# One 512-column matmul for both parts of an activation, in a hybrid RWKV-7, latent attention and ConvFFN layer

## The chip, the core and the metric

The kernel runs on one core of a Trainium2 chip. Its engines work side by side, each with an instruction queue of its own: TensorE (PE, with its weight loads PEld), VectorE (DVE), ScalarE (ACT), GpSimd (POOL) and SyncE (SP), which issues most DMAs. The metric is the device time of one execution in microseconds; lower is better. TensorE's granted clock is 2.4 GHz or 1.2 GHz; the profile shows it as 1.00 or 0.50.

## What is computed

One layer on 256 latent tokens and 256 context tokens of 2048 features. Cut to what matters here:

```python
def token_mixer(h, s0, ang, kv_prefix, P, emit):
    p = h @ P['w_in']
    p_rwkv, p_mla, p_gate = jnp.split(p, [RWKV_IN, RWKV_IN + MLA_IN], axis=-1)
    y_rwkv, s_fin = rwkv_branch(p_rwkv, s0, P, emit)
    k, v = mla_kv(p_mla, P, ang)
    ...
    o = blocked_attention(q, k_all, v_all).reshape(B, T, MLA_HEADS * V_HEAD)
    g_rwkv, g_mla = jnp.split(jax.nn.sigmoid(p_gate + P['gate_b']), N_BRANCH, axis=-1)
    merged = g_rwkv * (y_rwkv @ P['w_rwkv_proj']) + g_mla * (o @ P['w_mla_proj'])
    return merged @ P['w_out'], s_fin, (k, v)

def conv_ffn(h, P):
    u = depthwise_conv(h @ P['ffn_w_gate'], P['ffn_conv_w'], P['ffn_conv_b'])
    return (jax.nn.gelu(u, approximate=True) * (h @ P['ffn_w_val'])) @ P['ffn_w_down']

# the layer
x = x + g1 * rms_norm(out_lat, norm_mix_post)
h = modulate(rms_norm(x, norm_ffn_pre), sh2, sc2)
x = x + g2 * rms_norm(conv_ffn(h, P), norm_ffn_post)
```

## The kernel before

Features lie on partitions, tokens along the free axis: a product is 128 output features by 256 tokens in one PSUM bank, summed over K tiles of 128 input features. To keep float32 accuracy with the fast float32r matmuls, each operand is cut into two float32r parts, hi + lo. `weights` (line 151) loads up to 1024 weight columns (8 K tiles) by a DMA on SP and cuts each 512 of them, hi by a cast on ACT (line 186), lo by a subtraction on DVE (line 187), into a ring of five pairs of tiles `whi` and `wlo`. `gemm` (line 165) then issues three matmuls for a K tile: hi by hi (line 176), hi by the activation's lo (179), lo by hi (180). All products of the program go through `gemm`, but for the values of the attention (`values`, lines 902 to 904) and the heads' outputs (999 to 1001), which issue the same three by hand. The activations' parts are two separate tiles: `hc` and `hl` (normed context and latents), `ckv`, `cq`, `o`, `yg`, `mg`, `z`, `f`.

The stages, in order of time: `start` (modulation, first norm, the first seven units of 128 columns of `w_in`), then keys and values of the context, then `branches` (line 755): the other columns of `w_in`, the attention and its projection (`pm`) run in the foreground, and between their K tiles `pump` steps background generators, the RWKV pairs' three stages and, behind each pair, `finish` (line 714: group norm, which sends sums through DRAM and back). Then `merge` (`pr`, which reads the finished pairs back from DRAM as `yg`), the output projection (`project`, tile `o_ps`), `second_norm`, `ffn` (tile `pf`: 44 pairs of units, gate and value) and the down projection (`project` again). The order of each queue is made by a scheduler that simulates the program: an instruction's place follows from the order of the code and from when its operands are there in that simulation.

`second_norm` (line 1093) does not wait for the norm's 1/rms R: z is the residual stream x1 times the gains, without R, in two parts, with the modulation's shift as two more columns (so a matmul has 258). The six products of the first three pairs (`first`) start on it in quarters of K, while the sum of squares is made; `rst_pr` holds R on all partitions after two small matmuls, and ACT copies it to `R_o`. `ffn` multiplies each unit's columns by R (line 1157 or 1166) and adds the shift's column `col`:

```python
            pu, col = unit("w_fg", i)
            ...
            nc.vector.tensor_tensor(c, pu, R, ALU.mult)
            nc.scalar.activation(up[:, 1:257], c, AF.Identity, bias=col)
```

## Time and profile before

| | us |
|---|---|
| median of three runs | 2328.25 |
| lowest, highest | 2321.64, 2334.10 |
| span of the profiled execution (from its first to its last instruction) | 2325.7 |

The profile is of one execution. Its time is given as the span; what a run's time has beside the span is not in the profile. A group's "idle before" is the engine's idle time just ahead of its instructions, with the engine or DMA that ended it. Ends of matmuls are modelled and overlap the next one's start, so steps are taken from start to start; a stretch counts every instruction that lies in it in part.

### The profile page before, as it was taken

The page shows a single profiled execution, that of the slowest core. Times are in us where ns is not written, and L with a number is a line of the kernel's source. Part 1 is how long each engine was busy: PE and PEld are TensorE (multiplying, and loading weights), DVE is VectorE, ACT ScalarE, POOL GpSimd, SP SyncE. Part 2 cuts the span into 40 slices and gives each one's busy share as a digit, 9 for nine tenths or more (in the row PEclk, how much of TensorE's full clock was granted, in tenths as well). Part 3 has the DMA queues.
Part 4 walks back from the last instruction along what each step waited for, and adds up shares of the span by engine and source line. Part 5 has one row for each costly group of instructions (what it writes and reads, how often), then busy time and mean ns, then how long its engine had stood idle before and what let it go on. Part 6 is the DMA issues. An engine that isn't in the chain of part 4 may idle for free.

```text
span 2325.7 us, 50524 instructions
## 1 busy us (share of the span) xinstructions
PE 2225.3 (96%) x18728; PEld 2079.7 (89%) x18728; DVE 1542.7 (66%) x2970; ACT 1204.0 (52%) x2536; POOL 616.6 (27%) x1555
## 2 busy tenths in 40 slices
PE   5999989899999999999999999979999999999996
PEld 2788989898999998888877999979999999999996
DVE  5258677766756767777767457579686868655554
ACT  3244455555555556656655335546555555554442
POOL 0100016655655655465545000011010100000000
PEclk9999999999999999999999999989999999999998
DMA  9979787767767659778566578538575757556663
GB/s 349 317 232 304 234 280 229 226 190 215 231 192 220 212 163 305 247 245 266 174 195 178 172 234 294 176 112 281 182 254 182 254 175 246 181 178 184 188 185 111
DMA packets 250454, 511.39 MB, mean 220 GB/s; under 512 B 44800, under 2 KB 104208, under 8 KB 249568
## 3 DMA queue, kind: packets, MB, share of 16 engines
q1 hardware_dynamic: 246368, 501.88, 67.7%
q0 software_dynamic: 3840, 6.30, 1.1%
q8 instruction: 147, 2.41, 0.4%
q14 instruction: 99, 0.81, 0.1%
HBM read 455.54 MB, written 52.53 MB: 218 GB/s over the span
## 4 chain that ended last, share of the span: by engine, by line
PE 64%; DMA 5%; POOL 5%; DVE 3%; issue 2%; ACT 1%; SPq 0%; DVEq 0%; POOLq 0%; ACTq 0%
PE pf L176 7%; PE pf L179 7%; PE pf L180 7%; PE o_ps L179 5%; PE o_ps L176 5%; PE o_ps L180 5%; POOL Z L637 2%; POOL Zt L635 2%; PE g L180 2%; PE g L176 2%; PE g L179 2%; PE y_ps L708 1%; PE u_ps L691 1%; DMA lanes<-ti_d 1%; PE x_ps L685 1%
## 5 line engine op out<-in xcount | busy, mean ns | idle before, releaser
L187 DVE TENSOR_TENSOR wlo<-raw,whi 128x512 fp32r<-128x512 f32 x1072 | 740.1, 697 | 368.8 <-ACT whi L186 343.3
L186 ACT CAST whi<-raw 128x512 fp32r<-128x512 f32 x1072 | 654.2, 619 | 449.0 <-PE o_ps L179 135.5
L176 PE MATMUL pf<-z,whi 128*128 128x258 f32 x1408 | 401.8, 286 | 4.6 <-ACT z L1111 4.6
L180 PE MATMUL pf<-z,wlo 128*128 128x258 f32 x1408 | 399.5, 285 | 3.2 <-DVE wlo L187 3.2
L179 PE MATMUL pf<-z,whi 128*128 128x258 f32 x1408 | 400.9, 285 | 1.2 <-DVE z L1112 1.2
L176 PE MATMUL g<-hl,whi 128*128 128x256 f32 x1120 | 330.5, 295 | 1.1 <-ACT whi L186 0.6
L180 PE MATMUL g<-hl,wlo 128*128 128x256 f32 x1120 | 326.8, 293 | 1.6 <-DVE wlo L187 1.5
L179 PE MATMUL g<-hl,whi 128*128 128x256 f32 x1120 | 323.9, 289 | 0.0
L176 PEld LDWEIGHTS pf<-z,whi 128*128 128x128 f32 x1408 | 269.0, 191 | 4.9 <-ACT z L1111 4.9
L180 PEld LDWEIGHTS pf<-z,wlo 128*128 128x128 f32 x1408 | 267.9, 191 | 3.7 <-DVE wlo L187 3.7
L179 PEld LDWEIGHTS pf<-z,whi 128*128 128x128 f32 x1408 | 269.7, 192 | 1.5 <-DVE z L1112 1.5
L635 POOL TENSOR_TENSOR Zt<-Z,lanes 128x60 f32<-128x60 f32 (+24 forms) x496 | 194.2, 392 | 131.2 <-DMA lanes<-ti_d 71.5
L180 PEld LDWEIGHTS g<-hl,wlo 128*128 128x128 f32 x1120 | 218.5, 196 | 7.4 <-DVE wlo L187 2.6
L176 PEld LDWEIGHTS g<-hl,whi 128*128 128x128 f32 x1120 | 218.9, 195 | 6.3 <-issue 2.5
L179 PEld LDWEIGHTS g<-hl,whi 128*128 128x128 f32 x1120 | 219.0, 196 | 3.1 <-issue 1.2
L338 DVE SCALAR_TENSOR_TENSOR adacc<-araw,c,adacc 128x512 f32<-128x512 f32 x240 | 181.2, 755 | 53.5 <-DMA araw<-w_ada 51.7
L637 POOL TENSOR_TENSOR Z<-Z,Zt 128x60 f32<-128x60 f32 (+24 forms) x496 | 204.3, 412 | 36.0
L179 PE MATMUL o_ps<-f,whi 128*128 128x256 f32 x704 | 198.1, 281 | 0.0
L176 PE MATMUL o_ps<-f,whi 128*128 128x256 f32 x704 | 198.1, 281 | 0.0
L180 PE MATMUL o_ps<-f,wlo 128*128 128x256 f32 x704 | 198.1, 281 | 0.0
L1090 POOL TENSOR_TENSOR raw_o<-raw_o,R_o 128x1024 f32<-128x1024 f32 x2 | 4.7, 2347 | 489.6 <-ACT R_o L1083 489.6
L179 PEld LDWEIGHTS o_ps<-f,whi 128*128 128x128 f32 x704 | 132.5, 188 | 0.0
(327 smaller groups left out, 4826.7 us busy)
## 6 DMA issues: line engine op xcount, KB each, us to landing
raw<-w_in SPq DMA_DIRECT2D x150, 512.0 KB, 5.2
araw<-w_ada SPq DMA_DIRECT2D x256, 256.0 KB, 4.7
raw<-w_fg SPq DMA_DIRECT2D x82, 512.0 KB, 3.9
raw<-w_fv SPq DMA_DIRECT2D x82, 512.0 KB, 4.2
raw<-w_down SPq DMA_DIRECT2D x80, 512.0 KB, 3.7
araw<-w_ada SPq DMA_DIRECT2D x64, 512.0 KB, 6.0
raw<-w_mla SPq DMA_DIRECT2D x32, 512.0 KB, 4.7
raw<-w_out SPq DMA_DIRECT2D x32, 512.0 KB, 4.6
```

What stands on the lines that cost most here:

```text
L176: mm = nc.tensor.matmul(ps, wh, ahi[:, k], start=k == 0 and not shared, stop=False)
L179: nc.tensor.matmul(ps, wh, alo[:, k], start=False, stop=False)
L180: nc.tensor.matmul(ps, wl, ahi[:, k], start=False, stop=k == kt - 1 and (not shared or ps is segs[-1][0]))
L186: cut = self.nc.scalar.copy(hi, src)
L187: self.nc.vector.tensor_tensor(lo, src, hi.bitcast(F32), ALU.subtract)
L338: nc.vector.scalar_tensor_tensor(acc, raw, self.c1[:, k:k + 1], acc, ALU.mult, ALU.add)
L635: nc.gpsimd.tensor_tensor(tm[:, :m, j + 1:], Z[:, :m, j:j + 1].broadcast_to([128, m, t]), N[:, j:j + 1, j + 1:].broadcast_to([128, m, t]), ...
L637: nc.gpsimd.tensor_tensor(Z[:, :m, j + 1:], Z[:, :m, j + 1:], tm[:, :m, j + 1:], ALU.subtract)
L685: nc.tensor.matmul(px[64:128, u], XS[u // 2][:, c, u % 2], st[:, u], start=True, stop=True)
L691: nc.tensor.matmul(pu[64:128, u], vu[64:128, u], xv[64:128, u], start=True, stop=True)
L708: nc.tensor.matmul(o, st[64:128, u], rt[:, d, e, c], start=False, stop=True)
L1090: mul = eng.tensor_tensor(raw[:, c], raw[:, c], R.rearrange("p (o t) -> p o t", o=1).broadcast_to([128, 4, 256]), ALU.mult)
```

## The change

`hi` and `lo` of a weight become one tile `wc` of [128, 2, 512]. The two parts of an activation become one tile with, for each K tile, hi and lo side by side: [128, k, 2, 256]. A product's PSUM tile becomes 512 columns wide (it had half of a bank, now it has all). `product`, which `gemm`, `values` and `head` now call, looks at the widths: where PSUM is twice the activation it issues one matmul of 512 columns, weight hi by both parts, and one of 256, weight lo by the activation's hi, into the first half; otherwise the three matmuls of before. The latter holds for `start`'s units, for the three first pairs of up projections and for the keys `kn_ps`, whose activation has 512 tokens. `take` adds the two halves of a PSUM tile: a copy on ACT and an addition on DVE; every reader of a product now goes through it. `second_norm` still makes z, now in the end of the tile `f`, for the first three pairs, and then makes `h`, the normed and modulated input itself, in two parts: x1 times R (two quarters on DVE, two on POOL, into `raw`), times the gains plus the shift on DVE, and the split. The pairs from the fourth on read `h`, and need neither R nor the shift's column. The comments are taken out, so lines have other numbers. The core of the diff:

```diff
             pool, bufs = next(self.cuts)
-            hi = pool.tile([128, 512], F32R, tag="whi", name="whi", bufs=bufs)
-            lo = pool.tile([128, 512], F32R, tag="wlo", name="wlo", bufs=bufs)
-            cut = self.split(hi, lo, raw[:, o:o + 512])
+            w = pool.tile([128, 2, 512], F32R, tag="wc", name="wc", bufs=bufs)
+            cut = self.split(w[:, 0], w[:, 1], raw[:, o:o + 512])
             if HOLD and len(self.heads) >= HOLD:
                 self.behind(cut, self.heads[-HOLD])
-            yield hi, lo
+            yield w
...
-            for i, (hi, lo) in enumerate(self.weights(src[:, k0 * 128:(k0 + kn) * 128], kn * 128)):
-                for ps, ahi, alo in segs:
+            for i, w in enumerate(self.weights(src[:, k0 * 128:(k0 + kn) * 128], kn * 128)):
+                for ps, act in segs:
                     for j in range(4):
                         k = k0 + 4 * i + j
-                        wh, wl = hi[:, j * 128:j * 128 + 128], lo[:, j * 128:j * 128 + 128]
-                        mm = nc.tensor.matmul(ps, wh, ahi[:, k], start=k == 0 and not shared, stop=False)
+                        wh, wl = w[:, 0, j * 128:j * 128 + 128], w[:, 1, j * 128:j * 128 + 128]
+                        mm = self.product(ps, wh, wl, act[:, k], k == 0 and not shared, k == kt - 1 and (not shared or ps is segs[-1][0]))
                         if j == 0:
                             head = mm
-                        nc.tensor.matmul(ps, wh, alo[:, k], start=False, stop=False)
-                        nc.tensor.matmul(ps, wl, ahi[:, k], start=False, stop=k == kt - 1 and (not shared or ps is segs[-1][0]))
...
+    def product(self, ps, sh, sl, act, start, stop):
+
...
+        mm = self.nc.tensor.matmul
+        n = act.shape[2]
+        if ps.shape[1] == 2 * n:
+            m = mm(ps.rearrange("p (i n) -> p i n", i=2), sh, act, start=start, stop=False)
+            mm(ps[:, 0:n], sl, act[:, 0], start=False, stop=stop)
+            return m
+        m = mm(ps, sh, act[:, 0], start=start, stop=False)
+        mm(ps, sh, act[:, 1], start=False, stop=False)
+        mm(ps, sl, act[:, 0], start=False, stop=stop)
+        return m
+
+    def take(self, out, ps, rows=slice(0, 128)):
...
+        self.nc.scalar.copy(out, ps[rows, 0:256])
+        if ps.shape[1] == 512:
+            self.nc.vector.tensor_tensor(out, ps[rows, 256:512], out, ALU.add)
+
...
-        segs = [(self.psg.tile([128, 256], F32, tag="g", name="g"), *(self.hc if s == "c" else self.hl)) for s in seqs]
+        segs = [(self.psg.tile([128, 512], F32, tag="g", name="g"), self.hc if s == "c" else self.hl) for s in seqs]
         self.gemm(self.a["w_in"][t], KT, segs, pump=pump)
         return [s[0] for s in segs]
...
-        nc.scalar.activation(g, ps, AF.Tanh, bias=self.gbh[:, i:i + 1], scale=0.5)
+        self.take(g, ps)
+        nc.scalar.activation(g, g, AF.Tanh, bias=self.gbh[:, i:i + 1], scale=0.5)
         nc.sync.dma_start(self.gsc[i], g)
...
-            pr = self.psg.tile([128, 256], F32, tag="g", name="pr")
-            self.gemm(self.a["w_rwkv"][i], 8, [(pr, *yg)])
+            pr = self.psg.tile([128, 512], F32, tag="g", name="pr")
+            self.gemm(self.a["w_rwkv"][i], 8, [(pr, yg)])
             m = ep.tile([128, 256], F32, tag="mm", name="mm", bufs=2)
-            nc.vector.scalar_tensor_tensor(m, gt[:, 0], 1.0, pr, ALU.add, ALU.mult)
+            self.take(m, pr)
+            nc.vector.scalar_tensor_tensor(m, gt[:, 0], 1.0, m, ALU.add, ALU.mult)
             nc.vector.tensor_tensor(m, m, gt[:, 1], ALU.add)
-            nc.scalar.mul(self.mg[0][:, i], m, 0.5)
-            nc.vector.scalar_tensor_tensor(self.mg[1][:, i], m, 0.5, self.mg[0][:, i].bitcast(F32), ALU.mult, ALU.subtract)
+            nc.scalar.mul(self.mg[:, i, 0], m, 0.5)
+            nc.vector.scalar_tensor_tensor(self.mg[:, i, 1], m, 0.5, self.mg[:, i, 0].bitcast(F32), ALU.mult, ALU.subtract)
...
-            ps = self.psg.tile([128, 256], F32, tag="g", name="o_ps")
-            self.gemm(src[i], kt, [(ps, *act)])
+            ps = self.psg.tile([128, 512], F32, tag="g", name="o_ps")
+            self.gemm(src[i], kt, [(ps, act)])
             sq = acc if i == 0 else fo.tile([128, 256], F32, tag="sq_o", name="sq_o", bufs=2)
-            nc.scalar.activation(sq, ps, AF.Square)
-            nc.scalar.mul(raw[:, i], ps, gg[:, i:i + 1])
+            self.take(raw[:, i], ps)
+            nc.scalar.activation(sq, raw[:, i], AF.Square)
+            nc.scalar.mul(raw[:, i], raw[:, i], gg[:, i:i + 1])
             if i:
                 nc.vector.tensor_tensor(acc, acc, sq, ALU.add)
...
+        h = zp.tile([128, KT, 2, 256], F32R, tag="h", name="h")
+        self.split(z[:, :, 0, 256:258], z[:, :, 1, 256:258], self.mod[:, 0, 3].rearrange("p (k o) -> p k o", o=1).broadcast_to([128, KT, 2]))
         first = {(n, i): self.psg.tile([128, NZ], F32, tag="g", name="pf") for i in range(3) for n in ("w_fg", "w_fv")}
...
+        R = fo.tile([128, 256], F32, tag="R_o", name="R_o")
         nc.scalar.copy(R, pr)
-        return z, first, R
-
-    def ffn(self, z, first, R, f, fp):
+        for q in range(4):
+            c = slice(4 * q, 4 * q + 4)
+            t = raw[:, c]
+            (nc.gpsimd if q % 2 else nc.vector).tensor_tensor(t, self.x1[:, c], R.rearrange("p (o t) -> p o t", o=1).broadcast_to([128, 4, 256]), ALU.mult)
+            for k in range(4 * q, 4 * q + 4):
+                nc.vector.tensor_scalar(raw[:, k], raw[:, k], gs[:, k:k + 1], self.mod[:, 0, 3, k:k + 1], ALU.mult, ALU.add)
+                self.split(h[:, k, 0], h[:, k, 1], raw[:, k])
+        return h, first, R
+
+    def ffn(self, h, first, R, f, fp):
...
-                ps = self.psg.tile([128, NZ], F32, tag="g", name="pf")
-                self.gemm(self.a[n][i], 16, [(ps, *z)])
+                ps = self.psg.tile([128, 512], F32, tag="g", name="pf")
+                self.gemm(self.a[n][i], 16, [(ps, h)])
+                self.take(out, ps)
+                return
             col = fp.tile([128, 1], F32, tag="col", name="col", bufs=2)
             nc.scalar.copy(col, ps[:, 256:257])
-            return ps[:, 0:256], col
+            nc.vector.tensor_tensor(t, ps[:, 0:256], R, ALU.mult)
+            nc.scalar.activation(out, t, AF.Identity, bias=col)
...
-            pu, col = unit("w_fg", i)
             up = fp.tile([128, 258], F32, tag="up", name="up", bufs=2)
             nc.gpsimd.memset(up[:, 0:1], 0.0)
             nc.gpsimd.memset(up[:, 257:258], 0.0)
             c = fp.tile([128, 256], F32, tag="cv", name="cv", bufs=2)
-            nc.vector.tensor_tensor(c, pu, R, ALU.mult)
-            nc.scalar.activation(up[:, 1:257], c, AF.Identity, bias=col)
+            unit("w_fg", i, up[:, 1:257], c)
...
-            pv, col = unit("w_fv", i)
-            v = up[:, 0:256]
-            nc.vector.tensor_tensor(v, pv, R, ALU.mult)
-            nc.vector.scalar_tensor_tensor(c, v, col, c, ALU.add, ALU.mult)
-            self.split(f[0][:, i], f[1][:, i], c)
+            v = fp.tile([128, 256], F32, tag="v", name="v", bufs=2)
+            unit("w_fv", i, v, up[:, 0:256])
+            nc.vector.tensor_tensor(c, v, c, ALU.mult)
+            self.split(f[:, i, 0], f[:, i, 1], c)
```

The places at which the order of an engine's instructions moves are shown in five pieces. Numbers behind a name tell one buffer or unit from another. The first piece is PE before, where the first three pairs end (`pf_20457` is the sixth product) and the fourth pair's first unit (`pf_21028`) begins:

```order
L179 MATMUL pf_20457<-z1_20449,whi_20943 128x258
L180 MATMUL pf_20457<-z0_20448,wlo_20944 128x258
L225 MATMUL rst_pr_20959<-const_199,rst_yb_20849 128x128 x2
L176 MATMUL pf_21028<-z0_20448,whi_21031 128x258
L179 MATMUL pf_21028<-z1_20449,whi_21031 128x258
L180 MATMUL pf_21028<-z0_20448,wlo_21032 128x258
L176 MATMUL pf_21028<-z0_20448,whi_21031 128x258
L179 MATMUL pf_21028<-z1_20449,whi_21031 128x258
```

The second is PE at the same place in the change, `pf_18069` the sixth product, whose z lies in `f`, and `pf_18674` the fourth pair's first unit:

```order
L191 MATMUL pf_18069<-f_18058,wc_18532 128x258
L192 MATMUL pf_18069<-f_18058,wc_18532 128x258
L242 MATMUL rst_pr_18547<-const_199,rst_yb_18443 128x128 x2
L187 MATMUL pf_18674<-h_18061,wc_18677 128x512
L188 MATMUL pf_18674<-h_18061,wc_18677 128x256
L187 MATMUL pf_18674<-h_18061,wc_18677 128x512
L188 MATMUL pf_18674<-h_18061,wc_18677 128x256
L187 MATMUL pf_18674<-h_18061,wc_18677 128x512
```

What stood on z behind `rst_pr` now stands on `h`, two matmuls for a K tile instead of three. The third piece is DVE in the change behind the 1/rms (`rst_yb`), from the products with R (L1157) over gains and shift (L1159) to the splits (L204, where `h` is written):

```order
L238 COPY rst_yb<-rst_y 128x256
L204 TENSOR_TENSOR wc<-raw,wc 128x512
L1157 TENSOR_TENSOR raw_o<-x_17136,R_o 128x1024 x2
L1159 TENSOR_SCALAR raw_o<-raw_o,gs_18059,mod 128x256 x12
L204 TENSOR_TENSOR h<-raw_o,h 128x256 x5
L1159 TENSOR_SCALAR raw_o<-raw_o,gs_18059,mod 128x256 x2
L204 TENSOR_TENSOR h<-raw_o,h 128x256
L1159 TENSOR_SCALAR raw_o<-raw_o,gs_18059,mod 128x256
L204 TENSOR_TENSOR h<-raw_o,h 128x256 x6
L1159 TENSOR_SCALAR raw_o<-raw_o,gs_18059,mod 128x256
L204 TENSOR_TENSOR wc<-raw,wc 128x512 x2
L204 TENSOR_TENSOR h<-raw_o,h 128x256 x3
```

None of these rows but the cuts of weights (`wc`) was there before: there, `rst_yb` was followed by cuts and by the first units' products with R. The fourth piece is PE before, late in the branches: the second matmul of the last pair's `finish` (`mu_ps`) among the units of the attention's projection (`pm_18189` is the thirteenth of sixteen, in its fourth K tile):

```order
L179 MATMUL pm_18189<-o1_16959,whi_18192 128x256
L180 MATMUL pm_18189<-o0_16958,wlo_18193 128x256
L176 MATMUL pm_18189<-o0_16958,whi_18192 128x256
L726 MATMUL mu_ps_18138<-y1_18134,const_199 2x256
L179 MATMUL pm_18189<-o1_16959,whi_18192 128x256
L180 MATMUL pm_18189<-o0_16958,wlo_18193 128x256
L176 MATMUL pm_18189<-o0_16958,whi_18208 128x256
```

The fifth is the same matmul in the change (`pm_16374` is the fourteenth unit, in its first K tile):

```order
L188 MATMUL pm_16296<-o_15282,wc_16351 128x256
L187 MATMUL pm_16374<-o_15282,wc_16377 128x512
L188 MATMUL pm_16374<-o_15282,wc_16377 128x256
L744 MATMUL mu_ps_16253<-y1_16249,const_199 2x256
L187 MATMUL pm_16374<-o_15282,wc_16377 128x512
L188 MATMUL pm_16374<-o_15282,wc_16377 128x256
L187 MATMUL pm_16374<-o_15282,wc_16377 128x512
```

It moved behind by 13 K tiles of `pm`; the merge still follows the sixteenth unit.

## Rows read from the trace of the kernel before

**Rows 1.** The page, part 1: busy time, share of the span, instructions of each engine.
```profile
PE 2225.3 (96%) x18728; PEld 2079.7 (89%) x18728; DVE 1542.7 (66%) x2970; ACT 1204.0 (52%) x2536; POOL 616.6 (27%) x1555
```

**Rows 2.** Stretches: us, busy us (x instructions) of each engine, PEclk, DMA share, GB/s.
```profile
1390.00:1425.00 35.00, 35.00 (x294) 35.00 (x293) 29.96 (x65) 20.11 (x39) 0.00 (x0) 1.00 0.93 320
1600.00:2036.00 436.00, 436.00 (x3626) 436.00 (x3625) 327.95 (x596) 235.63 (x494) 36.44 (x118) 1.00 0.64 214
2042.00:2275.00 233.00, 233.00 (x1964) 233.00 (x1963) 121.83 (x185) 111.54 (x197) 0.56 (x1) 1.00 0.63 185
430.00:800.00 370.00, 365.21 (x3310) 338.88 (x3307) 256.88 (x490) 210.34 (x455) 220.65 (x525) 0.98 0.69 210
```

**Rows 3.** Timeline of PE, a run of 512-column matmuls: start us, us, what.
```profile
1081.88 0.40 PE L179 MATMUL kn_ps<-ckv,whi 128*128 128x512 f32 x1
...
1083.49 0.39 PE L180 MATMUL kn_ps<-ckv,wlo 128*128 128x512 f32 x1
```

**Rows 4.** Line 176 over the span as a stretch; groups of PE by form, xcount | busy us, mean ns.
```profile
0.00:2326.00 2326.00, 1279.99 (x4416) 848.25 (x4416) 0.98 0.69 220
...
L176 PE MATMUL pf<-z,whi 128*128 128x258 f32 x1408 | 401.8, 286 | 4.6 <-ACT z L1111 4.6
L176 PE MATMUL o_ps<-f,whi 128*128 128x256 f32 x704 | 198.1, 281 | 0.0
L176 PE MATMUL o_ps<-mg,whi 128*128 128x256 f32 x256 | 72.0, 281 | 0.0
L902 PE MATMUL v_ps<-whi,ckv 128*128 128x256 f32 x128 | 37.9, 298 | 0.0
L176 PE MATMUL kn_ps<-ckv,whi 128*128 128x512 f32 x64 | 26.2, 409 | 0.5 <-DVE ropet L889 0.5
L999 PE MATMUL o_ps<-cq,hd 128*128 128x256 f32 x64 | 22.9, 361 | 1.0 <-ACT cq L186 0.6
```

**Rows 5.** Timeline of the output projection's norm, and a stretch behind it (PEclk).
```profile
1526.71 0.42 PE L225 MATMUL rst_pr<-const,rst_yb 128*128 128x128 f32 x1
...
1527.58 1.22 DVE L1090 TENSOR_TENSOR raw_o<-raw_o,rst_pr 128x1024 f32<-128x1024 f32 x1 [1.72 <-ACT R_o L1083]
1527.68 2.34 POOL L1090 TENSOR_TENSOR raw_o<-raw_o,R_o 128x1024 f32<-128x1024 f32 x1 [229.19 <-ACT R_o L1083]
1528.83 2.27 DVE L1091 TENSOR_TENSOR x<-x,raw_o 128x1024 f32<-128x1024 f32 x1
1530.10 3.22 POOL L1091 TENSOR_TENSOR x<-x,raw_o 128x1024 f32<-128x1024 f32 x1
...
1528.00:1530.00 2.00, 0.00 (x0) 0.00 (x0) 1.97 (x2) 0.00 (x0) 2.00 (x1) 0.50 0.00 0
```

**Rows 6.** Groups of DVE by form: xcount | busy us, mean ns | idle before us <-releasers.
```profile
L187 DVE TENSOR_TENSOR wlo<-raw,whi 128x512 fp32r<-128x512 f32 x1072 | 740.1, 697 | 368.8 <-ACT whi L186 343.3 <-PE o_ps L179 15.5 <-PE g L179 0.8
...
L321 DVE TENSOR_SCALAR h<-x,gs,mod 128x256 f32<-128x256 f32 x16 | 6.9, 475 | 0.1
...
L1061 DVE SCALAR_TENSOR_TENSOR mg<-mm,mg 128x256 fp32r<-128x256 f32 x16 | 6.4, 418 | 0.0
...
L1124 DVE TENSOR_TENSOR raw_o<-raw_o 128x1024 f32<-128x1024 f32 x1 | 1.2, 1211 | 0.0
...
L477 DVE TENSOR_SCALAR stage<-stage 128x256 f32<-128x256 f32 x2 | 0.6, 277 | 0.0
```

**Rows 7.** Timeline of PE at the end of the branches, and a stretch behind it.
```profile
1354.43 0.38 PE L726 MATMUL mu_ps<-y,const 128*2 128x256 f32 x1
...
1382.77 0.55 PE L176 MATMUL pr<-yg,whi 128*128 128x256 f32 x1 [4.88 <-DMA yg<-ysc]
...
1384.00:1386.00 2.00, 2.00 (x12) 2.00 (x11) 0.00 (x0) 0.00 (x0) 0.00 (x0) 0.53 1.00 280
```

**Rows 8.** Groups of ACT and of DVE by form that read 256 columns of PSUM.
```profile
L1005 ACT COPY o<-o_ps 128x256 f32<-128x256 f32 x16 | 5.9, 371 | 9.8 <-PE o_ps L1001 9.5
...
L752 DVE TENSOR_TENSOR y<-y,g_ps 128x256 f32<-128x256 f32 x8 | 3.3, 418 | 1.7 <-PE g_ps L751 1.6
```

111 lines of the change are left out of this document (52 added, 59 removed).

## The prediction

> **What bounds the kernel now.** I read the page's busy line first: TensorE (PE) is busy 96% of a span of 2325.7 us, VectorE (DVE) 66% [rows 1]. Matmul records overlap, so a busy PE alone says little. The test is the step from one matmul's start to the next, and I took it from stretches in which PE does nothing but one kind of matmul. A stretch counts the matmuls that lie across its edges too, about two more than belong to it; with two taken off, 1600 to 2036 us, the feed-forward's up projections (`pf`, 258 columns), holds 3624 in 436 us: 120.3 ns each. 2042 to 2275 us, the down projection (`o_ps<-f`, 256 columns), holds 1962 in 233 us: 118.8 ns. 1390 to 1425 us, the merge (`pr`), holds 292 in 35 us: 119.9 ns. The clock is at its full 2.4 GHz in all three [rows 2]. The steps are even and no engine is waited for there, so the number of matmuls times their step is the time. The background work of 430 to 800 us fills DVE to 257 of 370 us and PE to 365 [rows 2], so PE is the bound there too, if with less to spare on the other engines.
>
> **The term that gains: one matmul fewer for each K tile.** A K tile (128 rows of a weight) now costs three matmuls of 256 columns, hi by hi, hi by lo, lo by hi. The change does the first two as one of 512. The columns are the same, 768 for a tile, so what can be saved is only what a matmul costs beside its columns. The trace has the 512-column matmul: the keys' `kn_ps`. From 1081.88 to 1083.49 us there are seven steps, 1.61 us, 230 ns each [rows 3], against 238 to 240 for two of 256. At 2.4 GHz 256 columns take 106.7 ns and 512 take 213.3; so 12 to 13 ns lie beside the columns in the short one and 17 in the long one: the long one pays for less than two.
>
> The Trainium skill, "TensorE: Matmul & The Clock Gate", section "Back-to-back issue gap", gives a step of N/2.4 + 2.5 ns at the full clock, by which 256 columns would take 109.2 ns, 512 take 215.8, and the merged matmul would save 2.5 ns of a tile. By that rule the gain over the 4224 tiles counted below would be an estimated 11 us. The trace disagrees, with 119 to 120 and 230 [rows 2, 3].
>
> How many K tiles: line 176 runs once for each, 4416 times [rows 4]. Off go 64 of `kn_ps`, which is already 512 wide for each part and stays [rows 4]; 7 x 16 x 2 = 224 of the first units in `start`, which stay; and 6 x 16 = 96 of the first three pairs of up projections, which stay. On come 128 of `v_ps` (line 902) and 64 of the heads' outputs (line 999) [rows 4]. That is 4224. The new tile I take at 230 + 119 = 349 ns.
> - Up projections: 1408 - 96 = 1312 tiles [rows 4], from 3 x 120.3 = 360.9 to 349 (two columns of each matmul go as well): 11.9 ns, 15.6 us.
> - Output and down projection: 256 + 704 = 960 tiles [rows 4], from 356.4 to 349: 7.4 ns, 7.1 us.
> - All the rest, 1952 tiles, from the merge's 359.7 to 349: 10.7 ns, 20.9 us.
>
> Sum: 43.6 us. Bounds by the step of the long matmul: 225 ns (its columns' 213.3 and no more beside them than the short one's 12) would add 5 x 4.2 = 21 us; 240, two singles, would take 10 x 4.2 = 42 of them away and leave 2. I take the 230 that the seven steps average.
>
> **What it costs, 1: the up projections wait for the normed input.** Now the pairs from the fourth on (unit 3 in the code's count from 0) read z, which is there before the norm's 1/rms is; R is applied behind the product. In the change they read `h`, which is made of x1, R and the shift after `rst_pr`. PE's order (first and second piece in the section on the change) has unit 3's first matmul on `h` right behind `rst_pr`, with nothing between them. DVE's order (third piece) has, behind R: two products of 1024, twelve tensor_scalars, and only then the first five subtractions that finish a tile of h. From `rst_pr` to DVE's first product on R the trace of the first norm shows 0.45 us (1526.71 + 0.42 to 1527.58) [rows 5]. A product of 128x1024 from SBUF takes 1.21 us alone and 2.27 beside POOL, which works on the same (2.34 and 3.22 us) [rows 5, 6], and POOL has the other two quarters here: I take 2.27, 4.5 us for two. A tensor_scalar of 256 takes 0.28 us, and 0.48 beside POOL [rows 6]: four at 0.48, eight at 0.28, 4.1 us. A subtraction 0.42 [rows 6]. The first tile of h is there 9.5 us after `rst_pr`. Fifteen subtractions (6.3), four tensor_scalars (1.1) and three weight cuts of 0.70 (2.1) stand before the last one [rows 6]: 19 us. PE does until then unit 3's first product and four tiles of its second, 20 x 0.349 = 7.0 us. Lost: 12 us. After an idle stretch the clock is at its lower level, 1.2 GHz (0.50 at 1528 to 1530 us, behind that norm [rows 5]); PE is then mostly paced by DVE, so I add 2: **14 us**. Bounds: nothing beside POOL slowed, 9 us; all of it slowed, 18. SP's queue has the load of `conv` behind the same tiles (it takes the place of `raw_o`), with weights behind it, but they are those of unit 4's second product, some 12 us of PE work away: nothing. ACT casts the sixteen tiles of h meanwhile, one for each of DVE's subtractions: hidden by them.
>
> **2: the end of the branches.** The last pair's `finish` ends in a chain of round trips through DRAM on which the merge waits: from its matmul on line 726 at 1354.43 to the first `pr` at 1382.77 us are 28.3 us, the last 4.88 of them PE's wait for `yg` [rows 7]. In the order of the change that matmul stands 13 K tiles later among the `pm` units (fourth and fifth piece). The 28 us behind it stay, so the wait grows by 13 x 0.349 = 4.5 us, plus a longer stretch at 1.2 GHz (0.53 at 1384 to 1386 [rows 7]): **6 us**. Bounds: 0, if the DMAs happen to be quicker with less beside them, to 9.
>
> **3: the sum of the two halves.** `take` is a copy on ACT (0.37 us) and an addition on DVE (0.42) [rows 8] for each unit. In the feed-forward it takes the place of the product with R and the addition of the shift, as many DVE operations as before. Elsewhere it is new, once for each product (some 200 of them by the code), 0.42 us each time on a DVE that is 69% busy; the cuts of weights stand in the same queue, and the work hides as long as they keep ahead. I take 2 us for it; bounds 0 and 10. At the end of the output and of the down projection nothing hides it: 2 x 0.8 = **1.6 us**.
>
> **Sum.** -43.6 + 14 + 6 + 2 + 1.6 = -20.0 us: 2305.7 of 2325.7 us of span. The three runs before have a median of 2328.25, from 2321.64 to 2334.10; the profiled execution's span lies 2.6 us below that median, which I read as what lies around it. The forecast is 2328.25 - 20.0 = **2308 us**, 0.9% faster.
>
> **The rivals.**
> - *Given back (2323 us).* The mechanism works, but the h step costs its bound, 18, the join 9 and the additions on DVE 10: -43.6 + 18 + 9 + 10 + 1.6 = -5. For it: DVE is the second busiest engine and gets new work in every unit before the merge. Against: DVE's work in the feed-forward does not grow.
> - *The background's chain, not PE, sets the branches (2328 us).* Then the tiles ahead of the merge (1952 less its own 128, 1824) gain nothing, 19.5 us less: -0.5. For: the matmuls of that stage have a background that hops between POOL, DMA and DVE. Against: 365 of 370 us of PE busy [rows 2].
> - *A merged matmul costs two (2350 us, slower).* The place is every K tile, the price the step of the 512 columns: at 240 ns the gain is 2 us against 23.6 of costs, +22. It decides from 235 ns for no change (each ns is 4.2 us) and from 237 for slower by 0.5%. For: no 512-column matmul of the trace alternates with a short one, and each changes its weights. Against: 230 [rows 3]. The Trainium skill's rule above leans this way: its estimated 11 us of gain against the same costs would be 2341 us.
> - *Better (2287 us).* The long step is 226 and the h step costs 10: 17 and 4 us more.
>
> **How the numbers follow.** Forecast 0.50; given back 0.17; the chain 0.12; two singles 0.07; better 0.14. About 0.5%, 11.6 us, is what a measurement of this kernel can tell from no change. Faster by more needs 2316.6 or less: most of the forecast's own spread (0.46) and all of the better case: 0.60. Slower by more, from 2339.9: the singles and a little of what spreads around the chain case: 0.09. The same: 0.31. The range leaves out the singles and the outer part of the better case: 2289 to 2329.
>
> **What would show it.** The down projection should take 349 ns for a pair instead of 356 for three, the up projections 349 instead of 361. PE should have a hole of 8 to 10 us right behind the second `rst_pr` and full pace some 20 us after it. The wait for `yg` should be near 10 us. I am wrong if the 512-column matmul alternating with one of 256 steps above 235 ns, or if PE shows new waits for `wc` (the cuts) in the branches.

## The result and the profile after

The change makes the kernel slower: 2345.49 us, median of four runs (2341.46 to 2350.40), against 2327.05 us (2321.64 to 2334.10) for the kernel before; the ratio is 1.0083, 95% interval 1.0058 to 1.0107. The prediction was 2308 us, with a range from 2289 to 2329. The profiled execution has a span of 2345.5 us, 19.8 more than before.

The page's busy line and four stretches of the changed kernel, to set beside [rows 1, 2] (us, busy us (x instructions) of PE, PEld, DVE, ACT, POOL, then PEclk, DMA share, GB/s):

```profile
PE 2196.6 (94%) x14504; PEld 1848.2 (79%) x14504; DVE 1629.4 (69%) x3220; ACT 1254.7 (53%) x2658; POOL 640.5 (27%) x1557
...
1415.00:1450.00 35.00, 35.00 (x201) 30.45 (x200) 33.91 (x78) 23.96 (x51) 0.00 (x0) 1.00 0.91 296
430.00:800.00 370.00, 351.82 (x2606) 295.00 (x2605) 264.41 (x514) 210.26 (x464) 216.50 (x503) 0.95 0.67 204
1640.00:2040.00 400.00, 400.00 (x2290) 350.86 (x2289) 311.41 (x574) 221.77 (x434) 51.39 (x114) 1.00 0.71 224
2082.00:2300.00 218.00, 218.00 (x1244) 191.06 (x1243) 117.81 (x183) 111.41 (x198) 0.00 (x0) 1.00 0.64 188
```

In the feed-forward PE is as full as before. In the branches (430 to 800 us) it now stands still for 18 of 370 us, before for 5, and its clock is 0.95 where it was 0.98.

To see where the time went I laid the two traces side by side by work done: the start of the first matmul of each K tile, 4608 in both, counted from 0. The same K tile is the same work of the foreground; the time between two of them holds what the background and the waits took as well. Each column is one execution. How far two executions can differ ahead of the merge shows in the trace of `late_only` (below), which has the matmuls and reads of before there: 1210 us from K tile 256 to 2112, where the table has 1201 for before.

| stretch, by K tiles | before, us | after, us | difference |
|---|---|---|---|
| up to 256: set-up, first units | 182.0 | 178.4 | -3.6 |
| 256 to 1536: columns of `w_in`, context's keys and values | 721.9 | 723.3 | +1.4 |
| 1536 to 1856: attention (latents, keys, queries, heads) | 353.8 | 378.6 | +24.8 |
| 1856 to 2112: its projection `pm`, wait for `yg` | 125.2 | 123.7 | -1.5 |
| 2112 to 2240: merge `pr` | 47.5 | 48.8 | +1.3 |
| 2240 to 2496: output projection and its norm | 101.4 | 101.1 | -0.3 |
| 2496 to 2624: the three first pairs, second norm, h | 57.8 | 71.2 | +13.4 |
| 2624 to 3904: up projections | 466.1 | 452.9 | -13.2 |
| 3904 to 4607: down projection | 250.3 | 246.8 | -3.5 |
| behind: last norm and output | 19.8 | 20.9 | +1.1 |

From the merge on the parts cancel, -1.2 us. Everything that was lost was lost before it: the branches should have gained some 19 us, and in these two executions they lost 24.7 from K tile 256 to the merge.

### The profile page after: what moved, and what is told of

Read it like the earlier page. It is cut to its first block, busy times and chain, and to the rows that moved or that the text cites. A ratio compares the mean times of both kernels' runs of the same rounds, so it can differ in the third digit from the quotient of the medians.

```text
span 2345.5 us, 42262 instructions
## 1 busy us (share of the span) xinstructions
PE 2196.6 (94%) x14504; PEld 1848.2 (79%) x14504; DVE 1629.4 (69%) x3220; ACT 1254.7 (53%) x2658; POOL 640.5 (27%) x1557
## 4 chain that ended last, share of the span: by engine, by line
PE 61%; DMA 9%; DVE 8%; POOL 7%; issue 3%; ACT 3%; SPq 1%; DVEq 0%; POOLq 0%; ACTq 0%
PE pf L187 13%; PE o_ps L187 10%; PE pf L188 7%; PE g L187 5%; PE o_ps L188 5%; POOL Z L655 3%; POOL Zt L653 3%; PE g L188 3%; DMA araw<-w_ada 2%; DVE wc L204 2%; PE pm L187 2%; PE pr L187 1%; PE y_ps L726 1%; DMA raw<-w_in 1%; PE y_ps L725 1%
## 5 line engine op out<-in xcount | busy, mean ns | idle before, releaser
L204 DVE TENSOR_TENSOR wc<-raw,wc 128x512 fp32r<-128x512 f32 x1072 | 740.7, 698 | 335.9 <-ACT wc L203 326.4
L203 ACT CAST wc<-raw 128x512 fp32r<-128x512 f32 x1072 | 654.7, 620 | 464.3 <-PE o_ps L188 122.7
L187 PE MATMUL pf<-h,wc 128*128 128x512 f32 x1312 | 461.7, 395 | 11.3 <-DVE h L204 11.3
L187 PE MATMUL g<-hl,wc 128*128 128x512 f32 x1008 | 375.0, 410 | 6.5 <-ACT wc L203 3.9
L188 PE MATMUL pf<-h,wc 128*128 128x256 f32 x1312 | 368.6, 283 | 0.0
L187 PEld LDWEIGHTS pf<-h,wc 128*128 128x128 f32 x1312 | 246.2, 189 | 66.8 <-issue 11.5
L188 PE MATMUL g<-hl,wc 128*128 128x256 f32 x1008 | 293.6, 293 | 0.8 <-DVE wc L204 0.8
L188 PEld LDWEIGHTS pf<-h,wc 128*128 128x128 f32 x1312 | 247.7, 189 | 2.0 <-DVE wc L204 0.3
L187 PE MATMUL o_ps<-f,wc 128*128 128x512 f32 x704 | 247.2, 393 | 0.0
L187 PEld LDWEIGHTS g<-hl,wc 128*128 128x128 f32 x1008 | 193.6, 193 | 50.3 <-ACT wc L203 4.2
L188 PEld LDWEIGHTS g<-hl,wc 128*128 128x128 f32 x1008 | 195.1, 194 | 6.7 <-DVE wc L204 2.5
L187 PEld LDWEIGHTS o_ps<-f,wc 128*128 128x128 f32 x704 | 132.2, 188 | 30.5
L188 PEld LDWEIGHTS o_ps<-f,wc 128*128 128x128 f32 x704 | 132.4, 188 | 0.0
```

What stands on the lines that cost most here:

```text
L187: m = mm(ps.rearrange("p (i n) -> p i n", i=2), sh, act, start=start, stop=False)
L188: mm(ps[:, 0:n], sl, act[:, 0], start=False, stop=stop)
L203: cut = self.nc.scalar.copy(hi, src)
L204: self.nc.vector.tensor_tensor(lo, src, hi.bitcast(F32), ALU.subtract)
```

## The terms that can be read from the trace of after

**The merged matmul.** The row of the down projection has 1244 matmuls; with two taken off that lie across its edges, 1242 in 218 us are 621 pairs of 351 ns. From K tile starts it is 351.1 against 356.0 before, and in the up projections 353.8 against 364.2, background in both. From start to start, in both stages, the long matmul takes 230.6 ns, where 230 was assumed, and the short one behind it 120.4 to 120.6, where 119 was: 13.6 us less in the up projections, 4.7 in the two others. The rival of two singles (240 ns) is out. The Trainium skill, "TensorE: Matmul & The Clock Gate", section "Back-to-back issue gap", gives N/2.4 + 2.5 ns for an isolated matmul at the full clock, 215.8 ns for 512 columns. The 230.6 measured in this stream disagrees.

**The step to h.** Timeline of the changed kernel behind the second `rst_pr` (start us, us, engine, line, operation, xcount, [idle before <- what ended it]), and two stretches there:

```profile
1599.45 0.60 PE L242 MATMUL rst_pr<-const,rst_yb 128*128 128x128 f32 x4
...
1600.50 4.50 DVE L1157 TENSOR_TENSOR raw_o<-x,R_o 128x1024 f32<-128x1024 f32 x2 [3.78 <-ACT R_o L1153]
1600.60 6.60 POOL L1157 TENSOR_TENSOR raw_o<-x,R_o 128x1024 f32<-128x1024 f32 x2 [35.50 <-issue]
1604.92 5.97 DVE L1159 TENSOR_SCALAR raw_o<-raw_o,gs,mod 128x256 f32<-128x256 f32 x12
...
1610.82 1.75 DVE L204 TENSOR_TENSOR h<-raw_o,h 128x256 fp32r<-128x256 f32 x5
...
1611.38 0.76 PE L187 MATMUL pf<-h,wc 128*128 128x512 f32 x1 [11.32 <-DVE h L204]
...
1603.00:1616.00 13.00, 4.62 (x15) 3.97 (x16) 13.00 (x29) 6.65 (x18) 4.20 (x2) 0.50 0.00 1
1616.00:1625.00 9.00, 9.00 (x52) 7.68 (x52) 7.91 (x17) 5.21 (x12) 0.77 (x5) 1.00 0.71 175
```

Two products of DVE beside POOL take 4.50 us, as twice the 2.27 of [rows 5] had it, but one of them takes 1.23 and the other 3.36; twelve tensor_scalars take 5.97, where 4.1 was put for them (why stands at the end). PE waits 11.3 us, and at 1616 us the clock, 0.50 until there, is back. The term was 14, the table has 13.4.

**The join.** The last pair's `mu_ps` starts at 1378.43 us, the first `pr` at 1403.82 behind a wait of 7.13 us. It did move 13 K tiles, but the chain behind it took 25.4 us where 28.3 were assumed to stay; from `pm`'s last K tile to `pr` it cost 2.2 us more than before, not 6.

**The additions on DVE.** Line 199 of the changed kernel up to the merge (busy us (x instructions) of DVE alone), and DVE's waits at it up to the merge (in total us, times, longest us):

```profile
0.00:1404.00 1404.00, 70.32 (x168) 0.97 0.73 229
...
DVE gt L199 <- ACT gt L197: 12.2, 13, 2.7
DVE stage L199 <- ACT stage L197: 8.3, 12, 1.5
DVE rp L199 <- ACT rp L197: 3.9, 2, 3.1
```

168 additions up to the merge are 70 us of DVE. Some 31 us more, 24 of them in the three rows shown, DVE stands at one of them until ACT's copy of the product is there, with the background's operations behind it in the queue.

**What PE waits for.** The longest stretch of the changed kernel in which no matmul of the foreground runs, between two units of `g` (rows of PE; some left out):

```profile
584.60 0.39 PE L187 MATMUL g<-hl,wc 128*128 128x512 f32 x1
...
590.47 0.68 PE L715 MATMUL s_ps<-TT,kb 128*64 128x64 f32 x8
591.08 1.19 PE L674 MATMUL m_ps<-z,AU 32*32 32x32 f32 x32
592.94 1.19 PE L680 MATMUL m_ps<-TT,z 32*32 32x32 f32 x32 [0.67 <-ACT z L675]
...
599.96 0.68 PE L715 MATMUL s_ps<-TT,kb 128*64 128x64 f32 x8
606.20 1.09 PE L703 MATMUL x_ps<-vs,xs 128*64 128x64 f32 x8 [5.56 <-DVE vs L718]
608.04 1.11 PE L709 MATMUL u_ps<-xv,TT 64*64 64x64 f32 x8 [0.75 <-ACT xv L705]
609.08 1.22 PE L242 MATMUL rst_pr<-const,rst_yb 128*128 128x128 f32 x4
609.96 0.77 PE L187 MATMUL g<-hl,wc 128*128 128x512 f32 x1
...
584.80:609.90 25.10, 18.12 (x182) 15.08 (x181) 21.55 (x53) 14.48 (x34) 6.49 (x17) 0.78 0.71 202
```

For 25 us PE has nothing but the background's steps: it is busy with them for 18.1 us and waits for 7.1, 5.6 of these once for DVE, at a clock of 0.78; DVE is busy for 21.6 of the 25. The longest such stretch before has 8.3 us. `branches` (line 755 before) gives each of 18 intervals a fixed share of the foreground and then steps the background until the interval's stages are done: where the foreground runs out first, this is what is left. The prediction's other sign, new waits for `wc` in the branches, hardly shows: PE waits 10.0 us for cuts from K tile 256 to the merge, before 5.4.

## The experiments

All ratios are against the kernel before on the same chip, with 95% intervals; 0.1% is 2.3 us. A difference between two kernels of the table has some 5 to 10 us to both sides.

| kernel | columns / attention merged | additions | order | ratio | interval |
|---|---|---|---|---|---|
| changed kernel | yes / yes | yes | own | 1.0083 | 1.0058 to 1.0107 |
| late_only | no / no | no | own | 1.0006 | 0.9989 to 1.0024 |
| copies_only | no / no | copies alone | own | 1.0005 | 0.9983 to 1.0027 |
| adds_only | no / no | yes | own | 1.0072 | 1.0050 to 1.0095 |
| no_adds | yes / yes | copies alone | own | 1.0041 | 1.0024 to 1.0058 |
| merge_cols | yes / no | copies alone | own | 1.0066 | 1.0040 to 1.0091 |
| merge_attn | no / yes | copies alone | own | 0.9990 | 0.9974 to 1.0007 |
| pin_noadds | yes / yes | copies alone | PE as before | 1.0023 | 1.0004 to 1.0043 |
| pin_after | yes / yes | yes | PE as before | 1.0092 | 1.0058 to 1.0126 |
| late_badorder | no / no | no | PE as no_adds | 1.0168 | 1.0139 to 1.0198 |
| pin_all | yes / yes | copies alone | all as copies_only | 1.0015 | 0.9997 to 1.0033 |
| pin_all_after | yes / yes | yes | all as three matmuls | 1.0056 | 1.0035 to 1.0077 |
| order_only | no / no | copies alone | all as no_adds | 1.0126 | 1.0099 to 1.0153 |
| skip | no / no, 200 matmuls fewer | no | own | 0.9957 | 0.9938 to 0.9977 |
| pin_skip | no / no, 200 fewer | no | all as late_only | 0.9982 | 0.9971 to 0.9994 |

All of these have the change from the merge on.

### Where the loss lies

`late_only` undoes the change ahead of the merge: PSUM tiles of 256 columns there, so that `product` issues three, and the readers read PSUM.

```diff
-        segs = [(self.psg.tile([128, 512], F32, tag="g", name="g"), self.hc if s == "c" else self.hl) for s in seqs]
+        segs = [(self.psg.tile([128, 256], F32, tag="g", name="g"), self.hc if s == "c" else self.hl) for s in seqs]
...
-        self.take(g, ps)
-        nc.scalar.activation(g, g, AF.Tanh, bias=self.gbh[:, i:i + 1], scale=0.5)
+        nc.scalar.activation(g, ps, AF.Tanh, bias=self.gbh[:, i:i + 1], scale=0.5)
```

> The change from the merge on alone (merge, output projection, feed-forward, down projection); keys and branches again with three matmuls for a K tile, their products read straight from PSUM. Theory (the changed kernel loses its time in the branches: it stands 21 us behind at the first matmul of the merge, and all that comes later nets -1): 2326 us, within 3 of before. Rival 1 (what is lost in the branches comes from the weights' two parts lying in one tile `wc`, which stays here): about 2345. Rival 2 (the late part does better when the branches do not push the weights' ring into it): 2318 or less.

1.0006: the loss is gone, and what is left of the change is worth nothing that is clear of noise. One tile `wc` for both parts of the weights is not the cause.

### Additions, copies, merging

`no_adds` and `adds_only` change `take`; `copies_only` is `adds_only` without its second operation.

```diff
 # no_adds
-        if ps.shape[1] == 512:
+        if ps.shape[1] == 512 and self.late:
             self.nc.vector.tensor_tensor(out, ps[rows, 256:512], out, ALU.add)
 # adds_only, on PSUM tiles of 256 columns
+        elif not self.late:
+            self.nc.vector.tensor_tensor(out, ps[rows, 0:256], out, ALU.max)
```

> The changed kernel, but up to the merge `take` leaves out the addition on DVE, so the product of weight hi and activation lo is missing there; ACT's copy stays. Theory A (the additions lengthen DVE's queue, in which the background's steps stand; without them the matmul saved in each K tile is worth its 10 ns again): branches 20 to 25 us shorter than before, 2303 to 2308 us. Theory B (the additions cost the 21 us, but the matmuls saved bring nothing, since the background's round trips and not PE set the branches): 2322 to 2328. Theory C (neither: the order in which the background now stands behind the foreground's cheaper K tiles leaves it uncovered, additions or not): 2338 to 2348.

> As late_only, but every product up to the merge is read as in the change: ACT's copy and an operation on DVE of the addition's size (a maximum of the product with its own copy, which changes nothing). Three matmuls for a K tile. Theory A and B (the additions on DVE cost the time): 15 to 25 us over late_only, 2340 to 2350. Theory C (the order of the background behind cheaper K tiles costs it): within 5 us of late_only.

> As late_only (three matmuls for a K tile up to the merge), but every product there is read as `take` does without its addition: by a copy on ACT first, gates and values and the attention's projection from that copy. Known: copies with additions (adds_only) 12.4 us over late_only; merged with copies (no_adds) 7.2 over. If the additions on DVE alone cost: within 3 us of late_only, and no_adds' 7 us come from the merging. If ACT's copies lengthen the round trips too: 4 to 8 us over, and merging as such is worth nothing either way.

ACT's copies cost nothing that shows (1.0005). The additions cost 15.6 us from copies_only to adds_only, which has 194 of them where the change has 168, and 9.8 us from no_adds to the changed kernel: **10 to 15 us**, each with some 7 to both sides. How they cost it, by their own time, by DVE's standing at them or by what they hold up behind them, no run separates. None of the three theories for no_adds was met: it lies between B and C, 9.5 us over before. So merging ahead of the merge, with no additions, does not gain 19 us; it costs 8 over copies_only.

### Is it the order?

The scheduler makes the order of each queue from its own simulation, in which a merged tile counts for less than three matmuls: counted in the order, the background's matmuls then stand later among the foreground's K tiles, and further than for 24 us of matmuls left out (skip). The mean shift over the 64 K tiles from the one named, against the same kernel with three matmuls:

| K tile | 768 | 960 | 1280 | 1408 | 1664 |
|---|---|---|---|---|---|
| no_adds | 14 | 29 | 52 | 43 | 9 |
| merge_cols | 14 | 29 | 56 | 51 | 5 |
| merge_attn | 0 | 0 | 5 | 0 | 14 |
| skip | 14 | 15 | 11 | 2 | 3 |

Three kernels hold PE's instructions, from K tile 256 to the end of the branches, in the order of another kernel: each matmul is put behind the one that precedes it there, without a semaphore.

```diff
+    def put(self, k, m):
+        i = self.at.get(k)
+        ...
+        if i - 1 in self.got:
+            self.b.behind(m, self.got[i - 1])
```

> As no_adds (merged matmuls everywhere, the additions of `take` left out up to the merge), but TensorE's instructions from K tile 256 to the end of the branches are held in the order of the kernel before: each background matmul behind the same K tile as there. Measured so far: no_adds 9.5 us over before, late_only 2.3 over. Theory C (the background stands 10 to 50 K tiles further behind in no_adds, and the foreground runs out before it): the loss goes and the matmuls saved count, 12 to 20 us below before. Theory B (the background's round trips through the other engines set the branches, wherever TensorE has them in its row): within 5 us of no_adds.

> The changed kernel itself, its additions on DVE included, with TensorE's order in that stretch held as before the change. Theory C alone: 15 to 20 us below the changed kernel, 0 to 5 over before. Theory B with additions that lengthen the round trips: within 5 us of the changed kernel, 14 to 20 over before.

> As late_only (three matmuls and direct reads up to the end of the branches), but with TensorE's order there held as in no_adds, the background 10 to 50 K tiles further behind. Theory C: the order alone costs time: 10 to 25 us over late_only. Theory B: within 5 us of late_only.

Both directions do not agree. The late order costs 38 us when three matmuls are put in it (late_badorder against late_only), so the order can cost much. But PE's old order gives the merged kernel back only 4 us without additions, which is within the noise, and with them nothing (pin_after). PE's order alone is not the cause, or not all of it.

`skip` asks the other question, whether less work on PE is worth anything here:

```diff
+        if not self.late and self.kn > 512 and self.kn % 8 == 3 and not stop:
+            mm(ps, sh, act[:, 1], start=False, stop=False)
+            return m
```

> As late_only, but from K tile 512 to the end of the branches the product of weight lo and activation hi is left out in every eighth K tile: 200 matmuls of some 120 ns fewer, 24 us of TensorE work, a little more than merging saves there; nothing else is touched, the reads stay direct. If TensorE sets the branches: 20 to 25 us below late_only. If the background's round trips do (theory B): within 6 us of late_only.

Neither: 11.4 us under late_only (6 to both sides), half of the 24. Less work on PE counts there in part.

`merge_cols` and `merge_attn` divide the merging.

> As no_adds (additions left out up to the merge, so the product of weight hi and activation lo is missing where tiles are merged; copies stay), but merged in the columns of w_in (`g`) alone; values, queries, heads and the attention's projection have three matmuls. Known: neither part merged (copies_only) 1 us over before, both (no_adds) 9.5 over. If the loss is made in the attention itself: 8 to 13 us below before here. If it is carried in from the columns by the late background: 5 to 12 over before, as no_adds.

> As no_adds, but merged in the attention (values, queries, heads and their projection) alone, with its additions left out; the columns of w_in have three matmuls. If the loss is made in the attention itself: 8 to 20 us over before. If it is carried in from the columns: within 4 us of copies_only, so 3 below to 5 over before.

All of the loss comes with the columns (1.0066, against 1.0005 with nothing merged); merging in the attention is worth -3.5 us or nothing. In the traces the time shows up in the attention. The stretch from K tile 1536 to 1856 in before, copies_only, merge_attn, merge_cols, no_adds and order_only, in this order (columns as above):

```profile
903.83:1257.60 353.77, 342.53 (x2812) 291.20 (x2810) 255.09 (x601) 219.48 (x546) 189.64 (x512) 0.99 0.71 225
...
900.30:1263.20 362.90, 348.38 (x2824) 298.10 (x2823) 256.21 (x596) 236.24 (x593) 190.78 (x518) 0.96 0.70 220
...
912.30:1267.40 355.10, 341.64 (x2560) 276.86 (x2557) 257.40 (x601) 235.35 (x591) 193.67 (x519) 0.98 0.71 225
...
894.90:1276.50 381.60, 365.70 (x2996) 311.67 (x2994) 257.61 (x601) 241.35 (x603) 194.81 (x538) 0.96 0.66 210
...
888.10:1270.60 382.50, 361.78 (x2692) 292.39 (x2690) 259.75 (x605) 239.74 (x598) 194.36 (x538) 0.95 0.67 211
...
892.90:1287.50 394.60, 366.14 (x2956) 312.37 (x2954) 259.45 (x606) 240.46 (x597) 193.52 (x540) 0.95 0.65 205
```

The three with the late order in the columns take 382 to 395 us here, the three others 354 to 363, and merge_cols has the same three matmuls for a tile in this stretch as copies_only. But a cut by K tiles counts the background where it falls. PE has 172 matmuls more here in merge_cols than in copies_only, all of the background, and 17 of the 19 us between the two are PE's busy time. The stretch so shows where the background went, not where the time was lost. That shows over the whole way from K tile 256 to 2112, where all of them have the same work but for the merging and the reads (one execution each; before, copies_only, merge_cols, no_adds, pin_all, which follows below, and the changed kernel; columns as above):

```profile
182.00:1382.80 1200.80, 1158.13 (x9864) 1053.41 (x9863) 826.34 (x1674) 660.41 (x1466) 541.17 (x1378) 0.98 0.72 223
...
182.70:1388.40 1205.70, 1158.19 (x9864) 1054.51 (x9863) 828.10 (x1674) 694.92 (x1571) 537.60 (x1378) 0.98 0.71 223
...
178.90:1402.30 1223.40, 1160.32 (x8619) 991.33 (x8618) 831.43 (x1678) 696.50 (x1573) 542.86 (x1380) 0.96 0.70 220
...
179.40:1391.80 1212.40, 1151.67 (x8075) 952.43 (x8073) 829.04 (x1673) 692.28 (x1563) 539.78 (x1380) 0.97 0.71 221
...
182.00:1380.60 1198.60, 1139.98 (x8071) 941.34 (x8071) 826.81 (x1674) 694.27 (x1563) 540.92 (x1378) 0.98 0.71 224
...
178.40:1403.80 1225.40, 1148.01 (x8074) 947.30 (x8074) 885.02 (x1841) 689.92 (x1565) 544.27 (x1380) 0.97 0.71 219
```

merge_cols has 1280 merged tiles, by 10.7 ns each 14 us less for PE. Yet PE is busy 2 us longer than in copies_only and stands still 16 us longer (63.1 us for 47.5), at a lower clock. From no_adds to the changed kernel it stands still 17 us longer (60.8, 77.4). A place in no_adds, where an interval's foreground is used up and PE has background alone, from one `v_ps` at 950.96 us to the next at 965.76 (columns as above):

```profile
951.20:965.80 14.60, 13.01 (x122) 10.34 (x121) 6.69 (x14) 8.18 (x21) 4.14 (x15) 0.65 0.38 111
```

PE is busy for 13.0 of the 14.6 us, but at a clock of 0.65. In before the longest such stretch of the attention is 4.9 us. Such a stretch alone does not make a kernel slower: skip, the fastest of the table, has one of 12.5 us.

The last four hold all five engines, up to the merge, in the order of another kernel with the same reads.

> As no_adds, additions left out up to the merge (the product of weight hi and activation lo is missing there), but up to the merge the instructions of all five engines are held in the order that the same kernel has with three matmuls for a K tile (copies_only's). If the order is the cause of no_adds' 9 us over before: the cheaper tiles count as skip's did, some half of their 20 us or more, 8 to 15 us below before. If merging delays the background in any order: 3 to 10 over, as pin_noadds and no_adds.

> Three matmuls for a K tile up to the merge and the reads of copies_only, but all five engines in the order that no_adds has. If the order is the cause: 20 to 45 us over before (the tiles now cost 361 ns where that order was made for cheaper ones; late_badorder, with TensorE's order alone, lay 41 over). If not: 0 to 5 over.

> The changed kernel with its additions, all five engines up to the merge in the order that the same kernel has with three matmuls and an operation of the addition's size at each place. If the order is the cause and additions cost some 12 us (adds_only against copies_only): 3 below to 4 over before, 15 to 20 below the changed kernel. If merging delays the background in any order: 14 to 24 over before, as pin_after.

> As skip (200 of the products of weight lo and activation hi left out up to the merge, 24 us), but all five engines up to the merge in the order that late_only has with all of them. If a held order turns any saving into waits: within 5 us of late_only, 3 below to 5 over before. If merged matmuls hold up the background by themselves: 8 to 14 us below before, as skip in its own order.

With every queue as for three matmuls, merging costs 2 us over copies_only instead of 8 (pin_all). With the additions too (pin_all_after) it is 12 over copies_only, 4 below what they cost with three matmuls. The order of no_adds costs 28 us if three matmuls are run in it (order_only against copies_only). So the order that the scheduler makes of merged tiles costs some 6 us here, twice over (no_adds against pin_all, the changed kernel against pin_all_after), each time about as large as its interval. That it is the columns' part of the order is likely from merge_cols, but no run holds that part alone.

What the order does not explain: with it held, some 19 us less matmul time bring nothing at all, while pin_skip keeps 5.6 of its 24. So a held order turns most of any saving on PE into waits. A like share of the 19 would be 4.4 us gained, and pin_all lies 2.3 over copies_only, pin_all_after 3.7 under adds_only, each with some 7 us to both sides: whether a merged matmul does some harm of its own beyond the order stays **open**.

A rival that no run holds fixed is TensorE's clock. Every execution has a mean granted clock; twice the share that is missing of it, times the span, is the time at 1.2 GHz. In the mean over a kernel's executions this is 115 us in copies_only, 120 in late_only, 128 in pin_all, 149 in order_only, 150 in no_adds, 153 in merge_cols and 163 in late_badorder (93 to 99 in before). A merged K tile takes 350 ns at 2.4 GHz and 640 at 1.2 (rows at the end), so the 22 us between pin_all and no_adds are, by estimate from these steps, up to 10 us of PE's work, and the order's price is 6; the 13 between copies_only and pin_all are up to 6. The late order may so cost through the clock as much as through waits; no run separates the two.

### The step to h, and a kernel that is faster than both

Three versions on top of late_only.

```diff
 # late_z5: the fourth and fifth pair read z too
+            if ps is None and i < 5:
+                ps = self.psg.tile([128, NZ], F32, tag="g", name="pf")
+                self.gemm(self.a[n][i], 16, [(ps, z)])
 # late_spread: i < 9, and h in the background, a K tile at every third step
+                self.bg.append(Task(self.normed(h, R, gs, fp), every=3))
...
+        for k in range(KT):
+            t, sh = fp.tile([128, 256], F32, tag="ht", name="ht", bufs=2), self.mod[:, 0, 3, k:k + 1]
+            nc.vector.scalar_tensor_tensor(t, self.x1[:, k], gs[:, k:k + 1], R, ALU.mult, ALU.mult)
+            nc.scalar.activation(h[:, k, 0], t, AF.Identity, bias=sh)
+            nc.vector.scalar_tensor_tensor(h[:, k, 1], t, sh, h[:, k, 0].bitcast(F32), ALU.add, ALU.subtract)
+            yield
```

> As late_only, with the step to h behind the second norm made another way: for each K tile one product on DVE of x1, gain and 1/rms, ACT adds the shift and rounds, DVE subtracts; nothing on POOL, no whole quarters ahead of the first tile. Theory (PE waits 11.3 us for h because whole quarters and all gains stand ahead of the first split): first tile 2 us behind 1/rms, last about 16, so 3 to 5 us less than late_only. Rival (the last tile, not the first, sets PE's wait; DVE has as much work in all): within 2 us of late_only.

0.9992 (0.9972 to 1.0013). The wait fell from 11.3 to 7.0 us, but not to 2: the scheduler put fifteen of the sixteen products ahead of the first split, as these rows of DVE show (products, then splits).

```profile
1587.81 6.03 DVE L1152 SCALAR_TENSOR_TENSOR raw_o<-x,gs,R_o 128x256 f32<-128x256 f32 x15 [3.78 <-ACT R_o L1149]
1593.76 6.02 DVE L1154 SCALAR_TENSOR_TENSOR h<-raw_o,mod,h 128x256 fp32r<-128x256 f32 x15
```

> As late_only, but the fourth and fifth pair of up projections read z with three matmuls and are multiplied by 1/rms behind, as the first three; h is read from the sixth pair on. Theory (PE's 11.3 us wait for h with the slow clock behind it is the whole 13 us that the second norm has lost; two pairs are 23 us of TensorE work, longer than h takes to make): 11 to 13 us below late_only, so 9 to 11 below before. Rival (DVE then has the readers of four products with 1/rms as well as h and is late for the cuts of the weights): 3 to 6 below late_only.

Less than even the rival's 3 us: 0.9998 (0.9976 to 1.0020), 1.9 us under late_only. PE's wait for h is gone, and a wait for the cuts of weights has taken its place (PE's waits from `rst_pr` to 1700 us, in late_only and then in late_z5: total us, times, longest):

```profile
PE pf L187 <- DVE h L204: 11.3, 1, 11.3
PE pf L188 <- DVE wc L204: 0.4, 1, 0.4
...
PE pf L192 <- DVE wc L204: 7.7, 4, 4.2
```

So DVE's queue was the resource, rather than the place of the first reader of h; the next version tests that.

> As late_only, but h is made one K tile at a time in the background of the fourth to ninth pair of up projections, one at every third four K tiles, and these pairs read z (three matmuls, 1/rms behind); h is read from the tenth pair on. Theory (late_z5 gained only 2.4 us because DVE made all of h in one go ahead of the cuts of weights: PE waited 10.8 us for cuts there): no wait for cuts; 13 us less than late_only, less 6 x 0.33 for the pairs that keep three matmuls: 10 to 12 us below late_only, 7 to 10 below before. Rival (DVE, at 75% in this stage, cannot take 13 us more in 70 us): 3 to 6 below late_only.

0.9969 (0.9952 to 0.9987), 2313.15 us against 2323.19: 8.6 us under late_only by the ratios, somewhat less than expected, and faster than both kernels. From `rst_pr` to 1700 us the list of PE's waits is empty. This is the change from the merge on, with h's 15 us of DVE work spread over six pairs instead of put in front of PE.

> As late_spread, and the attention's projection (`pm`, the 16 units ahead of the merge, with little background left) merged and read through `take` too: 256 K tiles at 10.7 ns are 2.7 us. Theory: 0 to 3 us below late_spread. Rival (the last pair's finish, in the background of these units, and not TensorE sets the merge's begin): 0 to 4 above it.

0.9969 (0.9950 to 0.9988): nothing more. Its 256 K tiles did take 4 us less in its trace (114.1 against 118.1), and from the last of them to `pr` it was 2.6 us longer: that is how the rival would look, in which the last pair's `finish` sets the begin of the merge.

## Why the prediction was wrong

- **The step that failed is the count of "all the rest, 1952 tiles" at full price, 20.9 us, resting on "365 of 370 us of PE busy" [rows 2].** A busy PE in the branches was read as a PE that sets the time there. It does in part: 24 us off PE gave 11 (skip), so half a price was there. But the foreground is also what covers the background's round trips, and the intervals hold a fixed share of it: in the traces from K tile 256 to the merge PE is busy 10 us less than before, and stands still 35 us more (77.4 for 42.7). Merged, with the reads' cost taken away, these tiles brought -2 us with the orders held and -8 with the scheduler's own, instead of +19. The chain rival named this mechanism, at 0.12 and with a floor of no gain; that a cheaper foreground could cost time, through the order that is made from it, was in none of the cases. Nor was the clock, which these tiles were all priced to have in full.
- **Cost 3, the additions, is a term mis-sized:** 2 us with bounds 0 and 10; 10 to 15 measured. The 168 operations of 0.42 us were counted rightly as work, and their cover was named as DVE's idle time. What was not counted is that an addition waits in DVE's queue for PE and ACT, some 31 us of standing with the background's operations behind it. That this standing is what costs is argued, not shown.
- The long matmul: right (230.6 ns for 230). 13.6 and 4.7 us for 15.6 and 7.1; the short one behind it took 1.5 ns more than was put for it.
- The h step: right in size (13.4 for 14), in part by luck: the hole was 11.3 us, not 8 to 10, and the full pace back 16.5 us behind `rst_pr`, not 20.
- The join: 2.2 us for 6, inside its bounds; the order moved as foreseen, the chain behind was 2.9 us shorter. The project tails: +1.1 at the end for 0.8.
- The merge gained nothing in this trace (+1.3 for -1.4), and now has DVE busy for 33.9 of 35 us, the addition included, where it was busy for 30.0 of 35 [rows 2]. In late_only's trace, with the same code there, it took 46.5 us, 1.0 less than before: the difference is one of executions.

Ahead of the merge the sum had -19.5 (1824 tiles at 10.7 ns), +2 and +6: -11.5. The runs show +18 there, from copies_only over pin_all and no_adds to the changed kernel: 2 for merged tiles in a held order, 6 for the order, 10 for the additions (16 where they were added to three matmuls), each with 6 to 7 us to both sides. The +24.7 of the two traces are one execution of each.

## What to carry to other kernels

A matmul saved is worth its time only where PE's work is the longest thing in the stretch; in a stretch where PE's own foreground is the cover for round trips through other engines, count a saving at half or at nothing until a run with some matmuls left out says otherwise. An addition that is put on an in-order queue can cost its waiting as well as its time, and what it blocks. When an order comes from a simulation, a change of prices re-deals all of it: hold the old order in one run and put the new order under the old work in another, and the price of the order can be read apart. And set the granted clock of the executions beside their times: the late order comes here with 22 to 43 us more at 1.2 GHz.
